# Recurrence of a two-block layer: the side work handed out two steps a round over fifteen rounds

## The chip, the cores and the metric

The kernel runs on one core of a Trainium2 chip. The metric is the device time of one execution in microseconds (us). The core has TensorE (PE, with its weight loads shown as PEld), VectorE (DVE), ScalarE (ACT), GpSimd (POOL) and SyncE (SP, which here issues most DMAs).

## What is computed

Two transformer blocks over 512 tokens of width 1024 run one after the other. The first one, cut to what matters here, is:

```python
h = _rms_norm(x, norm_mix_pre)
z = h @ w_in_first
attn = _rms_norm(_dilated_attention(q, k, v), attn_out_gain)      # 8 heads of 64
# _rwkv7: 8 heads of 64, a state per head, token after token
state = state * w_t - sa * b_t + v_t * k_t;  y = state @ r_t
rw = (groupnorm(y) + bonus) * gate
mixed = concatenate([attn, rw], axis=-1) @ w_out
x = x + _rms_norm(mixed, norm_mix_post)
x = x + _rms_norm(square(relu(rms_norm(x) @ w_ffn_up)) @ w_ffn_down, norm_ffn_post)
```

The second block (convolution, forgetting attention, cross attention, sixteen experts) follows on the first one's `x`; the change does not touch it.

## The kernel before

Projections in float32 are made of three matmuls each: weights and activations are split into a high and a low half (`wsplit`, L350 to 358: ACT copies the high half, DVE subtracts for the low half), and `mm_as` issues high by high, high by low and low by high (L380 to 382). A step of the product with `w_out` for 128 tokens and 512 columns is twelve such matmuls.

The recurrence is chunked: 64 tokens to a chunk, eight chunks to a pair of heads, four pairs. `rw_run` (L828 to 892) runs it in 19 rounds, `s` = 0 to 18, on two lanes: lane 0 takes pairs 0 and 2 in rounds 0 to 15, lane 1 pairs 1 and 3 in rounds 2 to 17. A chunk's step `rw_step` (L953 to 986) has four stages: the first three follow from each other by a handoff from TensorE to VectorE (copies of lines 971 and 974, state update of 979 or 981), and the new state starts the next round; the fourth writes the output (L985) and is issued a round later, as `late`.

Between the stages `fill` hands out other work, by generators that stop after each step. `preps` prepares a half pair's operands (`rw_prep`, four steps, in buffers of the tags `l` and `h`); two steps a round are handed out, so they end in round 11. `posts` normalises a finished half pair (`rw_post`, three steps, from round 4 on); after the first half of a pair `mark` puts it into `ready`. `side` is a chain of three things. First `attention`: 16 units of two heads and 128 queries, each of three steps (scores with softmax, transposes, values), worked off by `pipe` at most three units at a time; three of its 24 steps are done before the rounds, 21 are left. Then `wout_attn`, nine steps: a preparation (L696 to 706) and eight product steps for the attention's half of `w_out` (L707 to 713), each half of 512 columns starting with two weight splits into the tags `h` and `l`. Then `wout_rw((0, 1))`, the recurrence's half for tokens 0 to 255, which steps without work until `ready` holds four pairs (L677).

`RF` says, for the three calls of `fill` in a round, how many side steps, preparation steps and whether normalisation steps are handed out. Before, it is one side step in each call: three a round.

Buffers come in tags with fixed counts (`N1`: p 20, r 4, l 5, h 5, u 13, a 4), PSUM banks in tags too (`mm` 2, `acc` 1, `s` 1, `tp` 2, `q` 2). The builder puts the instructions of each engine into an order by a priority that follows the text and by readiness; buffers and banks are handed on as their users finish. Each engine then works its queue in that order.

Of the kernel before, what the change touches and what calls it, by code (L numbers as in the profile page):

```python
# [37 lines left out]
XD = 1  # L38
CY = (1, 1)
PN = ()  # L40
RF = ((1, 0, 0), (1, 1, 1), (1, 1, 1))
AH = (3, 14, 3.0, 3, 22, 6.0)
FP, FG = (0,), ((0,), (1, 2), (3,))
AS = 'mm'
# [134 lines left out]
def run(gen):  # L179
    for _ in gen:  # L180
        pass


def chain(*gens):
    for g in gens:
        yield from g
# [38 lines left out]
class Block:  # L225
# [602 lines left out]
    def rw_run(self, ar, be, kv, pc, gbd, xd, lora, rT, ready, side):  # L828

        zx, z21 = self.halves("z_x", 2)  # L830
        self.eng("mx").memset(zx, 0.0)
        self.eng("ma21").memset(z21[:, :256], 0.0)
        z = dict(x=[self.c4(zx)[:, 4 * j:4 * j + 4] for j in range(2)], a21=self.c4(z21)[:, 0:4])
        order = [(0, 0), (1, 0), (0, 1), (1, 1), (2, 0), (3, 0), (2, 1), (3, 1)]
        o, st, yT = {}, {}, {}

        def prep(k):
            p, f = order[k]
            sl = lambda a: self.c4(a)[:, 4 * f:4 * f + 4]
            return self.rw_prep(k, f, ar[p][:, 4 * f:4 * f + 4], sl(be[p]), sl(kv[p][:, 0]), sl(kv[p][:, 1]),  # L840
                                gbd[2 * p + f], xd[p * 4:p * 4 + 4], z, o.setdefault((p, f), {}))

        run(prep(0))
        run(prep(1))
        posts = []
        preps = chain(*[prep(k) for k in range(2, 8)])
        late = []

        def mark(p, f):
            if f == 0:  # L850
                ready.append(p)
            return
            yield

        def fill(n_side, n_prep, post):
            for _ in range(n_prep):
                next(preps, None)
            for g in list(posts) if post else ():
                if next(g, g) is g:
                    posts.remove(g)  # L860
            for _ in range(n_side):
                next(side, None)

        for s in range(19):
            now = []
            bank = self.ps("q") if s < 18 else None
            for lane, off in ((0, 0), (1, 2)):
                if 0 <= s - off < 16:
                    j = s - off
                    p, c = 2 * (j // 8) + lane, j % 8  # L870
                    if c == 0:
                        yT[p] = self.ut("yT")
                    now.append((p, c, self.rw_step(p, c, o[p, c // 4], st, yT[p], pc[p],
                                                   bank[:, lane * 128:lane * 128 + 128])))
            run_once = lambda a: [next(g, None) for _, _, g in a]
            run_once(now)
            fill(*RF[0])
            run_once(late)
            for p, c, _ in late:
                if c % 4 == 3:  # L880
                    if c == 3:
                        rT[p] = self.pt("rT", F32R)
                    posts.append(chain(self.rw_post(p, c // 4, yT[p], ar[p], kv[p], lora, rT[p]), mark(p, c // 4)))
            run_once(now)
            fill(*RF[1])
            run_once(now)
            fill(*RF[2])
            late = now
        run(preps)
        while posts:  # L890
            fill(1, 0, 1)
        run(side)
# [954 lines left out]
```

## Time and profile before

| what | us |
|---|---|
| median of 3 runs (1453.44 to 1454.4) | 1454.07 |
| the profiled execution, whole | 1445.03 |
| its span, first to last instruction | 1443.2 |
| PE busy in it | 1370.2 (95%) |
| DVE busy | 875.6 (61%) |
| ACT busy | 623.8 (43%) |
| POOL busy | 51.3 (4%) |

The profile is of one execution. Matmuls are pipelined and the ends shown are modelled, so a covered TensorE is not TensorE at its peak. The granted clock of TensorE is shown as a share of 2.4 GHz. The rounds of the recurrence lie between 208 and 392 us of the span. Tile names in the rows are the program's: `stp` is a recurrence step's buffer, `q` its PSUM bank, `ws` split weights, `aA` the attention's output, `rT` the recurrence's output, `wl` a weight tile as loaded.

### The profile page before, as it was taken

The page shows a single profiled execution, that of the slowest core. Times are in us where ns is not written, and L with a number is a line of the kernel's source. Part 1 is how long each engine was busy: PE and PEld are TensorE (multiplying, and loading weights), DVE is VectorE, ACT ScalarE, POOL GpSimd, SP SyncE. Part 2 cuts the span into 40 slices and gives each one's busy share as a digit, 9 for nine tenths or more (in the row PEclk, how much of TensorE's full clock was granted, in tenths as well). Part 3 has the DMA queues.
Part 4 walks back from the last instruction along what each step waited for, and adds up shares of the span by engine and source line. Part 5 has one row for each costly group of instructions (what it writes and reads, how often), then busy time and mean ns, then how long its engine had stood idle before and what let it go on. Part 6 is the DMA issues. An engine that isn't in the chain of part 4 may idle for free.

```text
span 1443.2 us, 21699 instructions
## 1 busy us (share of the span) xinstructions
PE 1370.2 (95%) x8366; PEld 1080.2 (75%) x8366; DVE 875.6 (61%) x2035; ACT 623.8 (43%) x1143; POOL 51.3 (4%) x45
## 2 busy tenths in 40 slices
PE   5999999998889999999999999999999998699996
PEld 5877776776588888888888887776788897466663
DVE  5347465646775145343367485997456566799875
ACT  5244235533334243232344414444432453487873
POOL 0000000000000000000000000000000000232211
PEclk9999999999899999999999999999999999699998
DMA  5322420121223233232242315222122345799984
GB/s 204 104 79 71 157 75 15 38 91 52 64 84 99 76 117 102 74 117 96 80 146 88 99 29 171 84 62 85 59 92 87 123 169 190 240 311 338 334 286 144
DMA packets 67759, 178.01 MB, mean 123 GB/s; under 512 B 17144, under 2 KB 18552, under 8 KB 67648
## 3 DMA queue, kind: packets, MB, share of 16 engines
q1 hardware_dynamic: 58676, 156.39, 32.7%
q0 software_dynamic: 3584, 10.10, 3.2%
q10 hardware_dynamic: 5388, 10.06, 2.0%
q8 instruction: 68, 1.11, 0.3%
q14 instruction: 43, 0.35, 0.1%
HBM read 163.12 MB, written 15.88 MB: 124 GB/s over the span
## 4 chain that ended last, share of the span: by engine, by line
PE 82%; DVE 10%; DMA 3%; ACT 2%; issue 2%; SPq 0%; DVEq 0%; ACTq 0%
PE mm L371 11%; PE mm L372 11%; PE mm L373 11%; PE mm L380 10%; PE mm L382 10%; PE mm L381 10%; PE q L966 3%; DVE ws L357 2%; PE mm L1720 2%; PE acc L537 1%; PE s L512 1%; PE tp L531 1%; DVE cacc L1112 1%; PE tp L917 1%; PE mm L917 1%
## 5 line engine op out<-in xcount | busy, mean ns | idle before, releaser
L357 DVE TENSOR_TENSOR ws<-wl,ws 128x1024 fp32r<-128x1024 f32 (+2 forms) x238 | 280.7, 1192 | 141.2 <-ACT ws L354 134.6
L354 ACT ACTIVATE ws<-wl 128x1024 fp32r<-128x1024 f32 (+2 forms) x238 | 244.3, 1034 | 176.3 <-PE mm L382 106.5
L371 PE MATMUL mm<-hT,ws 128*128 128x512 f32 (+3 forms) x872 | 314.7, 365 | 1.7 <-ACT qT L565 0.7
L372 PE MATMUL mm<-hT,ws 128*128 128x512 f32 (+3 forms) x872 | 314.4, 363 | 1.1 <-DVE hT L427 1.0
L373 PE MATMUL mm<-hT,ws 128*128 128x512 f32 (+3 forms) x872 | 313.0, 361 | 0.0
L371 PEld LDWEIGHTS mm<-hT,ws 128*128 128x128 f32 (+2 forms) x872 | 162.4, 188 | 30.1 <-ACT qT L565 1.4
L372 PEld LDWEIGHTS mm<-hT,ws 128*128 128x128 f32 (+2 forms) x872 | 163.2, 188 | 27.2 <-DVE hT L427 2.1
L373 PEld LDWEIGHTS mm<-hT,ws 128*128 128x128 f32 (+2 forms) x872 | 163.0, 187 | 24.9 <-DVE ws L357 0.2
L380 PE MATMUL mm<-ws,ff 128*128 128x512 f32 x256 | 100.0, 391 | 0.0
L382 PE MATMUL mm<-ws,ff 128*128 128x512 f32 x256 | 99.7, 389 | 0.0
L381 PE MATMUL mm<-ws,ff 128*128 128x512 f32 x256 | 99.6, 389 | 0.0
L1112 DVE SCALAR_TENSOR_TENSOR cacc<-sig,vec,cacc 128x507 f32<-128x507 f32 (+25 forms) x120 | 86.1, 733 | 1.6
L1067 DVE TENSOR_TENSOR ur<-ur 128x512 f32<-128x512 f32 x32 | 22.1, 692 | 82.3 <-ACT ff L1066 82.3
L380 PE MATMUL mm<-ws,eh 128*96 128x512 f32 x136 | 56.4, 415 | 1.1 <-ACT eh L423 1.1
L1063 ACT ACTIVATE ur<-mm 128x512 f32<-128x512 f32 x32 | 19.0, 594 | 87.1 <-PE mm L373 87.1
L382 PE MATMUL mm<-ws,eh 128*96 128x512 f32 x136 | 55.5, 408 | 0.7 <-DVE eh L424 0.6
L381 PEld LDWEIGHTS mm<-ws,ff 128*128 128x128 f32 x256 | 48.1, 188 | 9.9
L382 PEld LDWEIGHTS mm<-ws,ff 128*128 128x128 f32 x256 | 48.1, 188 | 10.0
L380 PEld LDWEIGHTS mm<-ws,ff 128*128 128x128 f32 x256 | 48.1, 188 | 9.9
L381 PE MATMUL mm<-ws,eh 128*96 128x512 f32 x136 | 54.7, 402 | 0.0
L521 ACT ACTIVATE sp<-sp,mx 128x128 f32<-128x128 f32 (+3 forms) x64 | 35.7, 558 | 30.2 <-DVE mx L519 30.1
L1086 DVE TENSOR_TENSOR f<-f,mm 128x512 f32<-128x512 f32 x24 | 16.4, 685 | 49.2 <-PE mm L382 49.2
(436 smaller groups left out, 2364.1 us busy)
## 6 DMA issues: line engine op xcount, KB each, us to landing
wl<-w_gu SPq DMA_DIRECT2D x68, 512.0 KB
wl<-w_p SPq DMA_DIRECT2D x60, 512.0 KB
wed<-w_ed SPq DMA_DIRECT2D x68, 256.0 KB
wl<-w_up SPq DMA_DIRECT2D x32, 512.0 KB
wl<-w_dn SPq DMA_DIRECT2D x32, 512.0 KB
wl<-w_out SPq DMA_DIRECT2D x16, 512.0 KB
x<-x SPq DMA_DIRECT2D x8, 512.0 KB
gram_d<-gb SPq DMA_DIRECT2D x8, 256.0 KB
```

The costliest lines, as they stand in the source:

```text
L354: nc.scalar.activation(hi, t, AF.Copy)
L357: eng.tensor_tensor(lo, t, f32(hi), ALU.subtract)
L371: nt.matmul(ps, wh[:, c0:c0 + m], ah[:, sl], start=k == 0, stop=False)
L372: nt.matmul(ps, wh[:, c0:c0 + m], al[:, sl], start=False, stop=False)
L373: nt.matmul(ps, wl[:, c0:c0 + m], ah[:, sl], start=False, stop=k == len(ws) - 1)
L380: nt.matmul(ps, ah[:, sl], wh, start=k == 0, stop=False)
L381: nt.matmul(ps, ah[:, sl], wl, start=False, stop=False)
L382: nt.matmul(ps, al[:, sl], wh, start=False, stop=k == len(ws) - 1)
L521: nc.scalar.activation(sps[h][:, :n], sps[h][:, :n], AF.Exp, scale=-1.0, bias=mxs[h][:, 0:1], accum_out=ls[h])
L917: nc.tensor.matmul(ps[a, c], lhs[a, c], rhs(a, c), start=True, stop=True)
L966: nc.tensor.matmul(ps[a], lhs[a], rhs[a], start=n == 0, stop=n == len(terms) - 1)
L1112: nc.vector.scalar_tensor_tensor(acc[:, d:], up[:, 0:S - d], w(30 - d), acc[:, d:], ALU.mult, ALU.add)
```

## The change

`RF` becomes two tables, and a round takes the first up to `s` = 14 and the second after. The first hands out no side step in the first call of `fill` and one in each of the other two; the second is the table of before. The preparation and normalisation steps are handed out as before.

```diff
-RF = ((1, 0, 0), (1, 1, 1), (1, 1, 1))
+RF = (((0, 0, 0), (1, 1, 1), (1, 1, 1)), ((1, 0, 0), (1, 1, 1), (1, 1, 1)))
...
             run_once(now)
-            fill(*RF[0])
+
+            fill(*RF[s > 14][0])
             run_once(late)
...
             run_once(now)
-            fill(*RF[1])
+            fill(*RF[s > 14][1])
             run_once(now)
-            fill(*RF[2])
+            fill(*RF[s > 14][2])
             late = now
```

The 30 steps of `attention` and `wout_attn` that are left for the rounds are so handed out in rounds 0 to 14 (two each) where it was rounds 0 to 9 (three each). The last attention step and the preparation of `wout_attn` fall into round 10, the product steps into rounds 11 to 14.

## Rows read from the trace of the kernel before

**Rows 1.** The page, busy time, share of the span and instructions of TensorE.
```profile
PE 1370.2 (95%) x8366; PEld 1080.2 (75%) x8366; DVE 875.6 (61%) x2035; ACT 623.8 (43%) x1143; POOL 51.3 (4%) x45
```
**Rows 2.** The timeline of VectorE: line 971 in rounds 0, 7, 11 and 15.
```profile
209.24 0.21 DVE L971 COPY stp<-q 128x64 f32<-128x64 f32 x1
...
287.52 0.23 DVE L971 COPY stp<-q 128x64 f32<-128x64 f32 x1
...
340.82 0.22 DVE L971 COPY stp<-q 128x64 f32<-128x64 f32 x1
...
365.25 0.22 DVE L971 COPY stp<-q 128x64 f32<-128x64 f32 x1
```
**Rows 3.** Busy time by stretch: length, then engines with instructions, granted clock, DMA.
```profile
208.50:287.50 79.00, 77.11 (x1069) 56.21 (x1066) 48.52 (x194) 44.91 (x130) 0.00 (x0) 0.98 0.10 29
287.50:340.80 53.30, 50.66 (x623) 39.66 (x621) 22.86 (x90) 18.70 (x41) 0.00 (x0) 1.00 0.25 77
340.80:365.20 24.40, 19.25 (x306) 14.10 (x304) 18.06 (x72) 7.63 (x22) 0.00 (x0) 1.00 0.14 45
365.20:391.70 26.50, 25.57 (x190) 18.40 (x190) 18.35 (x60) 8.60 (x19) 0.44 (x1) 0.81 0.26 81
391.70:405.00 13.30, 7.64 (x26) 5.79 (x27) 11.44 (x42) 3.56 (x7) 0.08 (x1) 0.74 0.20 54
405.00:465.00 60.00, 58.46 (x362) 52.13 (x362) 39.59 (x76) 29.20 (x48) 0.00 (x0) 1.00 0.25 80
```
**Rows 4.** Busy time by stretch: rounds 0, 7, 8 and 13 alone.
```profile
208.50:216.10 7.60, 7.60 (x118) 5.78 (x114) 5.33 (x22) 4.58 (x12) 0.00 (x0) 1.00 0.17 47
...
287.50:292.90 5.40, 5.40 (x130) 5.12 (x126) 3.67 (x25) 2.53 (x7) 0.00 (x0) 1.00 0.53 172
292.90:313.60 20.70, 19.23 (x178) 14.65 (x177) 8.23 (x30) 6.69 (x14) 0.00 (x0) 1.00 0.29 88
...
353.90:358.90 5.00, 3.93 (x68) 2.84 (x68) 3.45 (x16) 1.54 (x5) 0.00 (x0) 1.00 0.07 27
```
**Rows 5.** Groups by line, TensorE, 208.5 to 287.5: busy, mean ns, idle before.
```profile
L531 PE MATMUL tp<-ident,sp 128*128 128x128 f32 x74 | 13.2, 288 | 0.7 <-DVE stp L971 0.7
L537 PE MATMUL acc<-pt,vA 128*64 128x128 f32 x148 | 12.6, 283 | 0.0
...
L512 PE MATMUL mm<-kT,qT 64*128 64x512 f32 (+3 forms) x26 | 10.8, 495 | 0.0
L512 PE MATMUL s<-kT,qT 64*128 64x128 f32 (+3 forms) x24 | 9.6, 482 | 0.3 <-DVE mx L519 0.3
```
**Rows 6.** Busy time by stretch of the matmuls with `ws` alone: length, busy, clock.
```profile
365.60:375.90 10.30, 5.87 (x12) 0.50 0.16 51
378.00:380.00 2.00, 2.00 (x10) 1.00 0.54 213
```
**Rows 7.** Groups by line, TensorE, 287.5 to 340.8.
```profile
L380 PE MATMUL mm<-ws,aA 128*128 128x512 f32 x32 | 13.5, 426 | 0.7 <-ACT ws L354 0.7
L381 PE MATMUL mm<-ws,aA 128*128 128x512 f32 x32 | 13.1, 409 | 1.7 <-DVE ws L357 1.7
```
**Rows 8.** The timeline: weight splits on VectorE and ScalarE.
```profile
314.76 1.23 DVE L357 TENSOR_TENSOR ws<-wl,ws 128x1024 fp32r<-128x1024 f32 x1
...
323.52 1.06 ACT L354 ACTIVATE ws<-wl 128x1024 fp32r<-128x1024 f32 x1 [0.67 <-PE q L966]
...
337.45 1.05 ACT L354 ACTIVATE ws<-wl 128x1024 fp32r<-128x1024 f32 x1
```
**Rows 9.** Busy time by stretch, ahead of the fall of the clock.
```profile
355.00:365.00 10.00, 7.75 (x120) 5.45 (x118) 6.44 (x23) 3.23 (x9) 0.00 (x0) 1.00 0.01 2
```
**Rows 10.** The timeline of SP's queue: issue of loads of `w_out`, `x` and `w_up`.
```profile
166.76 7.69 SPq L347 DMA_DIRECT2D wl<-w_out  x4
...
200.84 0.43 SPq L264 DMA_DIRECT2D x<-x  x1
...
342.20 52.99 SPq L347 DMA_DIRECT2D wl<-w_up  x7
```

## Prediction

> **What bounds the kernel now.** I began with the page's busy times: TensorE is covered 95% of the span [rows 1], so a gain has to come out of stretches where it isn't covered or runs at half clock. The chain of work that ended last runs through the recurrence, so I cut the trace there. The state copies of line 971 mark the rounds: round 0 starts at 209.2 us, round 7 at 287.5, round 11 at 340.8, round 15 at 365.2 [rows 2]; numbers of rounds count from 0, as `s` does. The stage table [rows 3] then shows three kinds of rounds. Rounds 0 to 6 (79 us, three attention steps each) have TensorE covered 77.11 of 79.00. Rounds 7 to 10 (53.3 us), which hold the attention's output product, have 50.66 of 53.30. Rounds 11 to 14, which the side work has left, have 19.25 of 24.40, with the clock at 2.4 GHz and VectorE at 18.06. In rounds 15 to 17 the product of the recurrence's half runs (25.57 of 26.50), with a mean granted clock of 0.81. From 405 us on, TensorE is dense again (58.46 of 60.00) for the FFN. So whatever brings the end of the recurrence forward brings the end of the kernel forward by as much.
>
> The single rounds agree [rows 4]: round 13, with nothing but the recurrence and its normalisation, lasts 5.0 us with TensorE covered 3.93; round 7 takes 5.4 with 5.40 covered; round 0 takes 7.6, all covered; round 8, with a block of output products, 20.7. The recurrence's own chain needs about 5 us a round, and above that a round lasts as long as TensorE's work in it.
>
> **The change, part by part.** Nothing is added or removed: 21 attention steps and 9 steps of `wout_attn` are handed out two a round over rounds 0 to 14, not three a round over rounds 0 to 9. The attention steps now end in round 10, in whose last fill the output product is prepared; its eight product steps fall into rounds 11 to 14. From round 15 three a round are handed out as before, and since `wout_rw` must wait for all four halves of `rT`, which line 851 marks in round 15, its products keep their place in the order.
>
> *Rounds 0 to 6 lose a step each.* The attention matmuls there cover 13.2 + 12.6 + 10.8 + 9.6 = 46.2 us [rows 5], over 21 steps 2.2 us each. Seven leave (15.4 us) and rounds 7 to 10 take them in again: 0 as long as both kinds of rounds are TensorE's. That is the cover of this term; where it fails is the first rival. The key tiles of attention live some rounds longer in the tag of 13 small buffers, from which the recurrence's `stp` also comes; no row shows a wait for it. I bound fewer ready steps by the idle shares of rows 3: 1.89 of 79.00 (2.4%) with three steps, 2.64 of 53.30 (5%) in rounds 7 to 10; the difference over 79 us is 2.0 us. The other end is 0. I take the middle: **+1.0**.
>
> *The product's 96 matmuls leave rounds 7 to 10.* At 2.4 GHz ten such matmuls fill 2.00 us [rows 6], so a step of twelve is 2.4 us or a little more, and the eight are 20 to 26. The work only moves. But 0.7 + 1.7 = 2.4 us of idle stand before these matmuls, waiting for the split halves of the weights [rows 7]. That leaves with them: **-2.4**.
>
> *They arrive in rounds 11 to 14.* There 24.40 - 19.25 = 5.15 us are uncovered [rows 3]. Two things keep part of it empty. The split weights take buffers of the tags `h` and `l`, five each, of which the operands of four half-sequences hold four from round 2 to round 11 (each is prepared two rounds ahead or more and used for four): in the trace before, the split at 323.52 us waited for a recurrence matmul [rows 8]. So in the new order the second half of the first product's weights gets a buffer only when the first half of pair 2, used in rounds 8 to 11, is released in round 12. Until then only half of two steps can run (12 matmuls, 2.4 us) while both `mm` banks stand open; behind them in TensorE's queue wait the normalisation's matmuls, which nobody needs before round 15. The other 36 come in rounds 13 and 14. I take 70% of the 5.15 as filled, bounds 1 and 5.15: **-3.6**.
>
> *The weight stalls come back.* The second product's two splits now wait for the first product's last matmul, and `wout_rw`'s first two, which ran at 337.45 and later, a round-15 step worked off before round 11 began [rows 8], get no buffer before round 14. A split is 1.06 us on ACT [rows 8] and then 1.23 us on DVE [rows 8]; one pair exposed is 2.3 us. Lower bound 1.2 (half covered by the recurrence), upper 4.6 (two pairs): **+2.3**. VectorE, at 18.06 of 24.40 in rounds 11 to 14 and 18.35 of 26.50 after [rows 3], can hold them.
>
> *The half clock.* TensorE was covered 7.75 of 10 us over 355 to 365 [rows 9], and from 365.6 to 375.9 the clock stood at 0.50, 1.2 GHz [rows 6]. In that time ran 12 products of 512 columns; at full clock ten take 2.00 us, so at half they cost 0.2 us more each, 2.4 in all. If rounds 13 and 14 are filled with such products, this stretch stays at full clock. Bounds 0 (it falls elsewhere, for instance in round 12) and -4 (the small matmuls gain too): **-2.4**. The second stretch at half clock, near 400 us, belongs to the last normalisation and I leave it.
>
> The Trainium skill, "TensorE: Matmul & The Clock Gate", section "Why this matters for your kernels", says to keep TensorE busy to hold the full clock; the fall after 355 to 365 us agrees. The same rule warns against the change if rounds 11 and 12 stay thin; by it the fall would only come earlier and the term would be 0.
>
> *Queues.* The loads of the product's weights were issued at 166.76 us, long before the rounds, the last of the three reloads of `x` at 200.84 [rows 10]; moving their step costs SP nothing. The w_up loads, from 342.20 us on, wait for buffers freed by splits and may start some 25 us later. They are first used past 405 us, so this is 0, as long as the fourth comes before about 395; otherwise it is a load's time at the head of the FFN. ACT's evictions of the product move to rounds where ACT is busy 7.63 of 24.40: 0.
>
> **Sum**: 1.0 - 2.4 - 3.6 + 2.3 - 2.4 = -5.1 us. Against the profiled execution (1445.03 us, span 1443.2) that is 1439.9. The median of the runs, 1454.07, is 9 us above the profiled one; nothing in the sum scales with that, so I take the same 5.1 off it: **1449.0 us**. With all terms at their good ends it is 0 - 2.4 - 5.15 + 1.2 - 4 = -10.4 (1443.7), at their bad ends 2.0 - 2.4 - 1 + 4.6 - 0 = +3.2 (1457.3).
>
> **Rivals.** *First, slower: the thinner rounds don't shorten.* If rounds 0 to 6 are set by handoffs and not by TensorE's work (attention, operand preparation and normalisation share two `mm` and two `tp` banks in the order of the steps), a round that loses a 2.2 us step shortens by less, while rounds 7 to 10 still pay for theirs. Each microsecond of a step that is not given back costs 7 us over seven rounds. The point from which this decides is 5.1 / 7 = 0.73 us of the 2.2, a third; with two thirds lost (1.45 us) it is +10.2 - 5.1 = +5 us, **1459**. For it: the weight loads of TensorE are at 56.21 of 79.00 in these rounds against 52.13 of 60.00 in the FFN [rows 3], so covered time is not full time. Against it: only 1.89 us are uncovered, and rounds 0, 7 and 13 show rounds shrinking with their work [rows 4].
>
> [...]
>
> *Second, same: the room isn't reached.* The buffers hold the product back until round 13 and beyond, the filling falls to 1, the clock falls anyway: 1.0 - 2.4 - 1 + 2.3 = 0, **1454**. For it: five buffers, four held. Against it: in rounds 13 and 14 alone 36 matmuls are free to run.
>
> *Third, same: the change doesn't change the order.* The builder orders instructions by readiness as well as by the text (the round-15 split before round 11 [rows 8]). If it fills TensorE with whatever is ready, attention stays where it is: **1454**. Against it: the banks and buffers are given out in the order of the steps, and in the trace before, the products keep to their rounds.
>
> **How the numbers follow.** Forecast 0.60, first rival 0.18, second 0.12, third 0.10. About 0.2% (2.9 us) is what a measurement of this kernel can tell from no change. The forecast's own range, gains over 2.9 us only, is 1442 to 1451; the second and third rival lie within 0.2% of the time before, the first above it. So faster 0.60, same 0.22, slower 0.18. For 8 in 10 the range takes in all of same and most of the first rival: 1442 to 1458.
>
> **What would show it.** Right: line 971's copies reach round 11 near 315 us instead of 340.8 (rounds 0 to 6: 79 - 15.4 + 1; rounds 7 to 10: 53.3 - 24 - 2.4 + 15.4), the products with `aA` lie in rounds 11 to 15, rounds 11 to 14 are covered over 90%, the stretch at half clock before 376 us is gone or shorter, and the FFN begins about 5 us earlier. Wrong: rounds 0 to 6 longer than 9.8 us in the mean with more idle than 2.4% (first rival); products with `aA` still running past the last recurrence step, with waits for `ws` before them (second); round starts as before (third).

## The result and the profile after

| kernel | median, us | range, us | executions |
|---|---|---|---|
| before | 1454.24 | 1453.44 to 1456.16 | 4 |
| changed | 1436.36 | 1433.15 to 1439.74 | 4 |

The ratio is 0.9895 with a 95% interval of 0.9861 to 0.9929: the changed kernel is 17.9 us faster, where 5.1 were forecast. Two more timings of it, below, gave 0.9895 and 0.9844. The traced execution took 1433.15 us (span 1431.3), 11.9 less than the traced one of before, so the two traces don't show all of it.

Busy time by stretch of the changed kernel, as [rows 3] had it for the kernel before: rounds 0 to 6, 7 to 10, 11 to 14, 15 to the recurrence's last output copy (line 985 before, 986 here), and the start of the FFN. Columns: stretch, length, then PE, PEld, DVE, ACT and POOL with instructions, granted clock, DMA share and GB/s.

```profile
209.70:276.70 67.00, 66.23 (x975) 48.44 (x975) 39.55 (x172) 33.71 (x101) 0.00 (x0) 1.00 0.08 19
276.70:313.90 37.20, 37.20 (x598) 28.09 (x593) 24.57 (x99) 19.70 (x55) 0.00 (x0) 1.00 0.17 54
313.90:359.10 45.20, 43.17 (x420) 31.60 (x416) 24.09 (x93) 16.76 (x34) 0.00 (x0) 1.00 0.24 77
359.10:381.70 22.60, 20.87 (x178) 14.84 (x178) 18.48 (x55) 9.17 (x20) 0.48 (x1) 1.00 0.37 117
395.40:455.00 59.60, 58.05 (x361) 51.82 (x360) 38.90 (x75) 28.81 (x48) 0.00 (x0) 1.00 0.24 76
```

The rounds last 172.0 us against 182.5 before, both counted from the first state copy (209.2 us before; [rows 3] start 0.7 us earlier). TensorE is uncovered for 0.77 + 0 + 2.03 + 1.73 = 4.5 us of them, where it was 1.89 + 2.64 + 5.15 + 0.93 = 10.6, and the clock stands at 1.00 throughout in this trace. Two later traces of the changed kernel, from the runs below, have a short fall in round 11: that round lasts 9.7 us at a mean clock of 0.82 in both, not 8.3, and rounds 11 to 14 last 46.6 us at 0.96. Round 11 starts where the forecast had it (315), as VectorE's timeline shows; the line is one further down in the changed kernel. ScalarE's timeline shows the wait for a buffer that was forecast too: the second half of the product's weights is split only when a recurrence matmul of round 12 has released one.

```profile
313.89 0.21 DVE L972 COPY stp<-q 128x64 f32<-128x64 f32 x1
...
322.28 1.06 ACT L354 ACTIVATE ws<-wl 128x1024 fp32r<-128x1024 f32 x1 [0.28 <-PE q L967]
```

Round 11 is the one that this leaves thin (7.05 of 8.30), but no matmul of the product waits for its weights any more: the groups by line of TensorE in rounds 11 to 14, with the idle time before them in the last column, have 0.1 and 0.0 us where [rows 7] had 0.7 and 1.7.

```profile
313.90:322.20 8.30, 7.05 (x118) 5.53 (x114) 6.53 (x37) 2.40 (x7) 0.00 (x0) 1.00 0.52 160
```

```profile
L380 PE MATMUL mm<-ws,aA 128*128 128x512 f32 x32 | 13.8, 432 | 0.1
L381 PE MATMUL mm<-ws,aA 128*128 128x512 f32 x32 | 12.9, 403 | 0.0
```

### The profile page after: what moved, and what is told of

The parts are those of the page before. It is cut to its first block, busy times and chain, and to the rows that moved or that the text cites. A ratio compares the mean times of both kernels' runs of the same rounds, so it can differ in the third digit from the quotient of the medians.

```text
span 1431.3 us, 21684 instructions
## 1 busy us (share of the span) xinstructions
PE 1364.3 (95%) x8366; PEld 1073.1 (75%) x8366; DVE 874.6 (61%) x2035; ACT 623.3 (44%) x1143; POOL 52.6 (4%) x45
## 4 chain that ended last, share of the span: by engine, by line
PE 84%; DVE 9%; DMA 2%; ACT 2%; issue 2%; SPq 0%; DVEq 0%; ACTq 0%
PE mm L371 11%; PE mm L372 11%; PE mm L373 11%; PE mm L380 10%; PE mm L382 10%; PE mm L381 10%; PE q L967 3%; PE mm L1721 2%; DVE ws L357 2%; PE acc L537 2%; PE s L512 1%; PE tp L531 1%; DVE cacc L1113 1%; PE mm L918 1%; PE tp L918 1%
```

## The experiments

### The changed kernel in more executions

> The changed kernel itself, timed in five rounds beside the kernel before. The two traces differ by 10.5 us between round 0 and the last recurrence step and by about 2 us elsewhere; the medians differ by 17.9 us. Theory 1: the change is worth what the rounds show, and the rest is scatter between executions: a ratio near 0.992 (11 to 12 us). Theory 2: some 6 us more are gained outside the rounds, for instance by falls of the clock that the changed order spares: a ratio near 0.988, and a trace in which a stretch outside the rounds is shorter too.

The ratio came out at 0.9895 (0.9857 to 0.9932): 1436.26 us (1429.67 to 1439.87, 6 executions) against 1451.42 (1440.92 to 1457.86, 17 executions). That is nearer the number of theory 2, though the interval holds that of theory 1 too, and nothing in this trace is shorter outside the rounds. What stood out was the kernel before: its mean granted clock was 0.962 to 0.964 in the executions of 1451.4 to 1457.9 us that make up more than half, and 0.973 to 0.976 in the four quickest (1440.9 to 1446.1). The changed kernel had 0.974 to 0.980. So the traced execution of before, 0.974 and 1445.03 us, was one of the quick ones, and the next step was to trace another.

### The kernel before, traced twice more

> The kernel before once more, for a trace of an execution of the usual kind: 17 executions took 1440.9 to 1457.9 us, with mean granted clocks from 0.962 (1457.3, 1457.9) to 0.976 (1443.8), so the traced one (1445.03 at 0.974) is one of the quicker ones. Theory 1: in the usual execution the clock stays at half for most of the thin rounds 11 to 15, some 10 us ahead of 365 us; then the rounds 11 to 15 are longer than 36 us in this trace. Theory 2: the further half-clock stretches lie elsewhere (ahead of the recurrence, or in the second block), and the rounds are as in the first trace.

> The same kernel before a second time, for a second execution: the same two theories. The time and the granted clock should lie on the same line: about 1.1 us more for each 0.001 less clock.

The first took 1453.24 us at 0.966, the second 1446.47 at 0.969. Busy time by stretch, the first trace with the rounds as above, and then its clock around 345 us and in the second block; after that the same of the second trace:

```profile
209.20:287.40 78.20, 76.31 (x1050) 55.45 (x1049) 48.09 (x194) 44.59 (x129) 0.00 (x0) 0.98 0.10 26
287.40:340.60 53.20, 50.67 (x624) 39.73 (x622) 22.90 (x91) 18.76 (x41) 0.00 (x0) 1.00 0.25 77
340.60:373.90 33.30, 29.88 (x306) 21.72 (x302) 18.91 (x72) 7.58 (x22) 0.00 (x0) 0.57 0.11 34
373.90:398.00 24.10, 23.17 (x190) 16.93 (x190) 18.13 (x60) 8.59 (x19) 0.44 (x1) 0.89 0.27 87
...
335.00:345.00 10.00, 8.98 (x124) 6.68 (x123) 6.17 (x26) 4.52 (x11) 0.00 (x0) 1.00 0.15 48
345.00:379.00 34.00, 31.47 (x289) 23.04 (x290) 18.02 (x67) 7.49 (x21) 0.00 (x0) 0.50 0.11 34
1030.00:1060.00 30.00, 30.00 (x130) 23.77 (x130) 16.64 (x34) 10.53 (x15) 0.00 (x0) 0.89 0.22 74
```

```profile
340.90:374.20 33.30, 29.87 (x306) 21.71 (x304) 18.99 (x73) 7.63 (x22) 0.00 (x0) 0.57 0.12 34
374.20:398.40 24.20, 23.27 (x190) 16.99 (x190) 18.15 (x60) 8.61 (x19) 0.46 (x1) 0.89 0.27 87
345.00:379.00 34.00, 31.24 (x292) 22.81 (x289) 18.15 (x68) 7.49 (x21) 0.00 (x0) 0.51 0.11 37
1030.00:1060.00 30.00, 30.00 (x143) 23.72 (x142) 18.40 (x36) 13.23 (x19) 0.00 (x0) 1.00 0.22 74
```

Theory 1 holds. Up to round 11 all three traces of the kernel before agree within 0.5 us. Then the clock falls at 345 us, not at 365.6 as in [rows 6], and stays at 1.2 GHz for 34 us. Rounds 11 to 14 last 33.3 us against 24.4, and the recurrence's last output comes at 398.0, not at 391.7. Both of these executions did so. The mean clocks suggest that most of the 17 did (13 of them had 0.970 or less, as these two had; the first trace had 0.974), but only these were traced. Against this trace the changed kernel's rounds are 188.8 - 172.0 = 16.8 us shorter, about the difference of the medians. The second trace is the quicker one by 6.8 us; its rounds are as long (188.8 us), but it misses a fall in the second block (the last line of each fence) and one near 1406 us. That kind comes and goes in either kernel, and the one line of 1.1 us for each 0.001 does not hold across such cases.

### Only the product moved

```diff
-RF = (((0, 0, 0), (1, 1, 1), (1, 1, 1)), ((1, 0, 0), (1, 1, 1), (1, 1, 1)))
+RF = (((1, 0, 0), (1, 1, 1), (1, 1, 1)), ((0, 0, 0), (0, 1, 1), (0, 1, 1)),
+      ((0, 0, 0), (0, 1, 1), (1, 1, 1)), ((0, 0, 0), (1, 1, 1), (1, 1, 1)))
...
-            fill(*RF[s > 14][0])
+            fill(*RF[0 if s > 14 or s < 7 else 1 if s < 10 else 2 if s == 10 else 3][0])
```

(The other two calls likewise.)

> Attention three steps a round in rounds 0 to 6 as before; no side step in rounds 7 to 9; the preparation of the product in round 10 and its eight steps in rounds 11 to 14, two a round, as after. Theory 1 (the gain is the product's place: it fills rounds 11 to 14 and keeps the clock up): close to the changed kernel, 8 to 12 us below the kernel before, since rounds 7 to 10 lose all of the product's time. Theory 2 (the thinner attention rounds are the gain, because TensorE has recurrence and operand work left beside attention in rounds 7 to 10): rounds 7 to 10 are left with the recurrence's chain alone and stand idle for several us, and the kernel is less than 5 us below the kernel before.

1431.0 us (1428.39 to 1434.86), ratio 0.9864 (0.9819 to 0.9909). Theory 1 holds, with a gain of 20 us where 8 to 12 were expected. In its rounds 7 to 10, which have no side work but the product's preparation, TensorE is covered without a gap, and the rounds get that much shorter:

```profile
210.40:286.70 76.30, 74.90 (x1051) 54.21 (x1050) 45.45 (x190) 42.05 (x125) 0.00 (x0) 1.00 0.12 31
286.70:311.80 25.10, 25.10 (x522) 21.25 (x517) 19.28 (x78) 11.26 (x30) 0.00 (x0) 1.00 0.23 68
311.80:358.60 46.80, 44.87 (x422) 32.91 (x418) 24.23 (x94) 17.09 (x35) 0.00 (x0) 0.96 0.19 57
358.60:381.20 22.60, 20.91 (x178) 14.85 (x178) 18.40 (x55) 9.15 (x19) 0.41 (x1) 1.00 0.37 118
```

The 101.4 us of rounds 0 to 10 compare with 104.2 after, the 69.4 from there to the recurrence's last output with 67.8 (69.2 in the two later traces). Spreading attention, the half of the change that its text names first, brings nothing by itself. The pair was timed again on one chip:

> The run with attention three a round as before and only the product moved to rounds 11 to 14, in five rounds beside the changed kernel on one chip. Theory 1 (only the product's place counts): within 3 us of the changed kernel. Theory 2 (the early end of attention, at 283 us instead of 304, gives something more): 3 to 6 us below the changed kernel, as the first timing had it (1431.0 against 1436.3).

> The changed kernel beside it: 1434 to 1438 us by both theories, 15 to 18 us below the kernel before in its usual state of the clock.

1432.3 us (1427.24 to 1438.12) and 1432.14 (1428.1 to 1436.5), ratios 0.9848 (0.9819 to 0.9877) and 0.9844 (0.9819 to 0.987) to 1453.04. The changed kernel came out below the 1434 to 1438 us expected of it, 20.9 us below the kernel before. By these times the two kernels can't be told apart, and the 5 us between them in the first timing were not found again. The traces do show a difference. Rounds 0 to 10 of the kernel with only the product moved, then rounds 0 to 10 and 11 to 14 of the changed one:

```profile
209.10:310.50 101.40, 100.00 (x1563) 75.45 (x1563) 64.77 (x267) 53.26 (x155) 0.00 (x0) 1.00 0.14 41
```

```profile
206.70:310.90 104.20, 103.43 (x1564) 76.51 (x1563) 64.12 (x267) 53.41 (x156) 0.00 (x0) 1.00 0.12 32
310.90:357.50 46.60, 44.55 (x420) 32.58 (x418) 24.18 (x93) 16.78 (x34) 0.00 (x0) 0.96 0.24 75
```

The same matmuls take 2.8 us more when attention is handed out as the change does it, and covered time holds all of that. It is 101.4 in both traces of the one kernel and 104.2 in all three of the other, too little for the medians to show.

### The product three steps a round

```diff
-            fill(*RF[s > 14][0])
+            fill(*RF[s > 10][0])
```

> Attention two steps a round to round 10 as after, then the product three steps a round: done in round 13, not 14. Theory 1 (rounds 11 to 14 only need enough work to be covered, and the buffers of the split weights set the product's pace anyway): within 3 us of the changed kernel. Theory 2 (every round needs its own share): round 14 stands half empty again, and 3 to 5 us of the gain are lost.

1439.34 us (1436.05 to 1449.81, 10 executions), ratio 0.9933 (0.9903 to 0.9962). By its trace it is theory 2: the product now ends before round 14, and that one round is enough. TensorE is covered 4.93 of its 6.60 us, the clock falls behind it, and rounds 15 to 17 need 26.4 us where they were 22.6. From round 11 to the last output it takes 74.9 us, where the traces of the changed kernel have 67.8 and 69.2. The median is 3.1 us above the changed kernel's in the same timing, which by itself would be no more than the scatter seen between timings.

```profile
353.10:359.70 6.60, 4.93 (x72) 3.49 (x72) 5.26 (x19) 2.13 (x5) 0.00 (x0) 1.00 0.56 163
359.70:386.10 26.40, 25.57 (x190) 18.40 (x190) 18.25 (x59) 8.59 (x19) 0.44 (x1) 0.81 0.25 80
360.00:370.00 10.00, 10.00 (x62) 7.41 (x59) 5.97 (x16) 3.04 (x7) 0.00 (x0) 0.50 0.16 50
```

### Another call left empty

```diff
-RF = (((0, 0, 0), (1, 1, 1), (1, 1, 1)), ...
+RF = (((1, 0, 0), (1, 1, 1), (0, 1, 1)), ...
```

> Two side steps a round to round 14, but the call left empty is the third one (after stage 3), not the first one (between stage 1 and stage 2). Theory 1 (the number of steps in a round matters, not their place): within 3 us of the changed kernel. Theory 2 (the step taken out stood in TensorE's queue between stage 1 and stage 2, so the recurrence's chain is what became shorter): the rounds are as long as before while attention lasts, and half of the gain or more is lost.

1432.83 us (1430.61 to 1436.1), ratio 0.9877 (0.9832 to 0.9922): nearer theory 1, since none of the gain is lost; the time lies 3.4 us below the changed kernel's. Its rounds 0 to 10 need 3.0 us less than the 104.2 of the changed kernel, as little as with three steps a round, and rounds 15 to 17, with a fall of the clock, take most of that back (25.30 us against 22.6):

```profile
209.90:311.10 101.20, 100.77 (x1571) 75.52 (x1569) 64.36 (x275) 54.25 (x156) 0.00 (x0) 1.00 0.13 37
356.70:382.00 25.30, 23.04 (x186) 16.80 (x182) 19.23 (x63) 9.29 (x19) 0.44 (x1) 0.93 0.31 102
```

So it is the empty first call, not two steps a round, that goes with the 2.8 us above; why is open. Put together with the product alone:

```diff
-      ((0, 0, 0), (0, 1, 1), (1, 1, 1)), ((0, 0, 0), (1, 1, 1), (1, 1, 1)))
+      ((0, 0, 0), (0, 1, 1), (1, 1, 1)), ((1, 0, 0), (1, 1, 1), (0, 1, 1)))
```

> The run with attention as before and the product alone in rounds 11 to 14, now with the product's two steps of a round in the first and second call, not in the second and third. Theory 1 (the number of steps in a round matters, not the call): 1429 to 1435 us like the two kernels it is made of. Theory 2 (the gains of the two add up): under 1429 us.

1434.6 us (1434.03 to 1436.18), ratio 0.9868 (0.9836 to 0.99): as theory 1 had it, the gains of the two don't add up.

### Useless work in the thin rounds

The kernel before, with nothing moved:

```diff
+        nc = self.nc
...
             run_once(now)
+            if 11 <= s <= 14:
+                dps = self.ps("s")
+                for p, _, _ in now:
+                    for h in range(2):
+                        nc.tensor.matmul(dps[0:64], st[p], kv[p][:, 1], start=True, stop=True)
             fill(*RF[0])
```

> The kernel before with work added: in rounds 11 to 14, after stage 1, four matmuls of 512 float32 columns with the state as weights into a PSUM bank that nobody reads. Nothing is moved. Theory 1 (what the thin rounds cost is the clock that falls in and after them): the half-clock stretch before 376 us is gone in the trace, the mean clock is 0.973 or more, and the kernel is faster than before by 3 to 10 us although it computes more. Theory 2 (what they cost is only uncovered time, into which moved work fits): the added work doesn't take anything off the rest, and the kernel is as long as before or up to 8 us longer (four rounds with about 2 us each).

1458.56 us (1447.87 to 1460.47), ratio 1.0023 (0.9996 to 1.005): no gain, and a time as theory 2 had it. In the trace the clock did hold through rounds 11 to 14, so theory 1 was half right, but the added 13.8 us were too much to tell the price of the clock from that of the work. Lighter versions, without the loop over `h`, and with `now[:1]` besides:

> As the run with added matmuls, but half of them: one 512-column float32 matmul a lane and round in rounds 11 to 14 (two instructions of about 0.43 us each), 6.9 us of added work in all. In the heavier run 13.8 us of added work made rounds 11 to 14 some 10 us longer than in the trace at full clock (34.4 against 24.4) and 1.1 us longer than in the usual one at half clock (33.3). Theory 1 (the fall of the clock in the thin rounds costs 6 us or more by itself): the clock holds through rounds 11 to 14, these last about 29.5 us, and the kernel is 2 to 5 us faster than before although it computes more. Theory 2 (the clock costs nothing, since the recurrence's chain sets the rounds): 4 to 7 us slower than before.

> The same with one added matmul a round (0.86 us, 3.4 us in all). Theory 1: if the clock still holds, rounds 11 to 14 last about 27 us and the kernel is 4 to 7 us faster than before; if it falls, 0 to 3 us slower, and the trace shows the fall. Theory 2: 1 to 3 us slower, whatever the clock does.

1448.39 us (1439.79 to 1450.9), ratio 0.9959 (0.9937 to 0.9982), and 1445.8 (1440.87 to 1450.82), ratio 0.9965 (0.9933 to 0.9997). Theory 1 in both: with work added that nobody reads, the kernel is faster, if by little. The lightest version's ten executions fall into two groups, five of 1440.9 to 1443.3 us at 0.975 to 0.980 and five of 1448.3 to 1450.8 at 0.972 or 0.973; the traced one (1443.31) is of the quicker group. Rounds 11 to 14 of the three, heaviest first, and rounds 15 to 17 of the lightest:

```profile
342.40:376.80 34.40, 32.72 (x347) 17.47 (x347) 18.37 (x68) 7.91 (x23) 0.00 (x0) 1.00 0.11 32
```

```profile
340.50:367.90 27.40, 25.58 (x328) 15.34 (x328) 17.93 (x67) 7.69 (x23) 0.00 (x0) 1.00 0.14 40
```

```profile
339.00:364.00 25.00, 22.18 (x323) 14.45 (x323) 17.78 (x68) 7.92 (x23) 0.00 (x0) 1.00 0.14 44
364.00:390.70 26.70, 24.80 (x194) 18.23 (x190) 18.58 (x64) 8.49 (x19) 0.48 (x1) 0.87 0.25 80
```

The lightest has these rounds in 25.0 us, 3.4 of added matmuls among them, against 33.3 at half clock. Its clock falls later, in rounds 15 to 17 (26.70 us at 0.87 against 24.10 at 0.89). Over both stretches that is 51.7 against 57.4.

## Why the prediction was wrong

The mechanism was right and its direction too; sizes were wrong, above all that of the half clock. Point by point:

- **The order moved as forecast.** Round 11 came at 313.9 (315 forecast); rounds 0 to 10 gave back 27.4 us (25.4 forecast). The third rival (order unchanged) is out. The first (thinner rounds don't shorten) isn't borne out: rounds 0 to 6 lasted 67.0 us, 9.6 each with 1.1% uncovered, and over rounds 0 to 10 two steps a round, with the third call empty, take no longer than three. But rounds 0 to 6 gave back only 11.3 of 15.4 us (78.3 to 67.0), in part because 73 of their 272 attention matmuls left them, not a third, 91. Some 1.4 of the 11.3 are another thing: a fall of the clock in round 3 (0.88 over 237.5 to 251.6 us of the first trace), which all three traces of the kernel before have. The kernel with only the product moved has the same work in these rounds without that fall, and 74.90 us covered where the usual execution of the kernel before has 76.31. Rounds 7 to 10 came out shorter than forecast (37.2 us, 42.3 forecast).
- **Thinner rounds, +1.0.** Sized by the wrong figure. Uncovered time in rounds 0 to 10 went from 4.53 to 0.77 us, 3.8 less; 2.4 of that were the weight stalls that were to leave, so by idle time the term was -1.4. What handing out attention this way did cost, 2.8 us against the kernel with only the product moved, was in covered time (103.43 against 100.00), which the term left out. That covered time is not full time, as the first rival had it, is seen here.
- **Filling, -3.6, and stalls that come back, +2.3.** Rounds 11 to 14 went from 5.15 to 2.03 us uncovered, -3.1. The wait for a buffer came as forecast, at 322.28 us, but no matmul of the product stood idle for it (0.1 us): behind it TensorE had the recurrence and the normalisation. What it did was to leave round 11 thin, which then lost 1.4 us to the clock in the two later traces (9.7 us against 8.3). The +2.3 never came; rounds 15 to 17 had 0.8 more uncovered. All terms of uncovered time (1.0 - 2.4 - 3.6 + 2.3) were to give -2.7; they gave 4.5 - 10.6 = -6.1 against the first trace.
- **The half clock, -2.4.** This is the step that failed. Against the first trace the covered time fell by 10.5 - 6.1 = 4.4 us, beyond the term's bound of -4. Against the usual execution, the trace at 1453.24 us, the rounds are 16.8 us shorter; covered time fell from 180.04 to 66.23 + 37.20 + 43.17 + 20.87 = 167.47, by 12.6, and uncovered time from 8.8 to 4.5. The 12.6 is a net figure: it holds the 1.4 of round 3, and the 3.4 of covered time that the new order added are already taken off it. The term counted 12 products in 10.3 us at half clock, from the one execution of three whose clock stayed full until 365.6 us. The usual one has 34 us at half clock, and with it 53.05 us covered from round 11 on instead of 44.82.
- **The sum.** "The median of the runs, 1454.07, is 9 us above the profiled one; nothing in the sum scales with that" was the error in words. Most of the 9 us were the same stretch at half clock, and the change takes it away: 6.3 of the 8.2 us between the first trace and the one at 1453.24 lie in the rounds. Even against its own trace the sum was short, 5.1 for 10.5: 2.4 by the thinner rounds, 2.3 by the stalls and 2.0 by the clock, less 0.5 by the filling and 0.8 in rounds 15 to 17.
- **The second rival** (the room isn't reached, the clock falls anyway) is out, since rounds 11 to 14 were filled to 43.17 of 45.20 us. Its second half is seen in the version with three product steps a round: where round 14 is left thin, the clock does fall behind it.

What is shown: the clock falls in the thin rounds in two of three traces of the kernel before and right behind them in the third (the mean clocks suggest the same of most executions); with matmuls added there it holds through them, and the fall by itself costs more than 3.4 or 6.9 us of such work does; moving the product alone into them gives the whole gain. What stays open is why the fall starts at 345 us in one execution and at 365.6 in another, and why leaving out the first call costs 2.8 us of covered time.

## What to carry to other kernels

When the traced execution is quicker than the median by more than the change is expected to bring, find out first in what state of the clock it ran: the trace may lack the very stretch that the change repairs. In this kernel a stretch of small dependent matmuls after a dense one cost twice, by its uncovered time and by the half clock in it and behind it; moving dense work that has no due time into it took most of both away, and covering most of it wasn't enough, as the one thin round 14 showed (26.4 us for rounds 15 to 17 instead of 22.6). Where the work was taken from and how it was handed out mattered little: up to 3 us over rounds 0 to 10, in covered time, which a look at idle time alone doesn't show.

## What the hardware showed beyond that

The same instructions at the same times (within 0.5 us) up to 345 us led to a clock that fell at 345 us in two executions and at 365.6 in a third. The Trainium skill ("TensorE: Matmul & The Clock Gate", Part 1) says that the chip judges activity in a window that runs on its own and doesn't start with the kernel, so that one kernel can differ from run to run. The three traces differ in that way, which agrees, but no run here shows where such a window stood. The price here is 6.3 us, 188.8 us for the rounds against 182.5. A fall in the second block is just as optional: 1030 to 1060 us stood at 0.89 in one trace of the kernel before and at 1.00 in the other, with TensorE covered for all 30 us in both, and no run here tells why.
